# Keys and queries placed by transfers from banks read at full height, and weight sums issued beside the first group

## The chip, the cores and the metric

The kernel runs on one core of one Trainium2 chip, as one launch. The metric is the device time of that core in microseconds, taken as the median of several executions; lower is better. The kernel before took 1184.37 us (median of 3 runs, 1184.14 to 1184.73).

A core has TensorE (PE in the profile), VectorE (DVE), ScalarE (ACT), GpSimd (POOL) and SyncE (SP). They run beside each other and wait for one another through semaphores. Each executes its own instructions in the order in which the program has them, so an instruction that waits holds up everything behind it on its engine. Transfers are issued by SP, ACT or POOL and run by 16 DMA engines.

## What is computed

A trunk of two layers over 1024 tokens of width 1024, all in float32. Each layer is a normalisation with a scale and a shift that depend on a conditioning vector (adaLN), a token mixer, and a gated residual. The reference, cut to the mixers:

```python
def even_mixer(h, ...):                       # layer 0
    qa, ka, va, ga, cq, ckv, kr, gb = split(h @ w_in)
    # first group: 8 query heads over 2 key heads, head size 64, dense softmax
    oa = dense_gqa_attention(axial_rope(rms_norm(qa)), axial_rope(rms_norm(ka)), va)
    # second group: 8 heads, keys and values from a latent of width 128
    qb = rms_norm(cq) @ w_uq                  # 64 columns without, 32 with rotation, per head
    q_lat = einsum('bshd,chd->bshc', q_nope, w_uk)
    ob = mla_attention(q_lat, rope(q_rope), rms_norm(ckv), rope(kr), w_uv)
    return concat([oa * silu(ga), ob * silu(gb)]) @ w_out

def odd_mixer(h, ...):                        # layer 1
    qc, kc, vc, gc = split(h @ w_in)          # 16 query heads, 4 key heads, head size 64
    # each block of 128 queries sees keys at most 128 tokens away, with a distance penalty and a sink
    return (windowed_sink_attention(qc, kc, vc, sink, slopes) * silu(gc)) @ w_out
```

After layer 1 comes a last normalisation.

## The kernel before

**Precision.** A matmul takes float32r, a shorter format than float32. Each operand is therefore held as a high part (its rounding, written by a copy with a float32r output) and a low part (the rest, by `sub`, line 641), and a product is made of three matmuls (`mm3`, line 644: high x high, high x low, low x high). So a projection's PSUM bank is read twice: by a copy on ACT for the high part, and by a subtraction on DVE for the low part.

**Keys and queries at half height.** A head has 64 dimensions, and a tile has 128 partitions. The projection of a pair of heads fills a bank of 128 partitions by 512 tokens: the even head in partitions 0 to 63, the odd head in 64 to 127. The score matmuls get their several products into one contraction by stacking high and low parts in the two halves of a tile, so each part is needed in particular halves of particular tiles. The kernel before writes each of these places straight from the bank, 64 partitions at a time:

- `b_heads` (line 1397), second group, per pair of heads and half of the tokens: three copies on ACT, one on POOL (`K2E`, line 1391) and two subtractions on DVE for the keys (lines 1409 to 1414), and as many for the queries (lines 1420 to 1425). The rotated part of the queries is brought back from DRAM (`qr_sp`) by transfers that POOL issues (lines 1401, 1402).
- `k_ft` (line 1783) and `q_ft` (line 1802), layer 1: four copies and four subtractions for a pair of keys, two and two for a pair of queries.
- `win_PV` (line 1887) adds the two halves of the attention output in four DVE operations of 64 x 128 (line 1906) into `og1`, which has one tile per pair of heads.

**Attention of layer 0.** `run_groups` (line 1183) walks 32 groups: 16 of the first group (head h, half of the queries; `Pa`, `hla` in the profile), then 16 of the second (`Pb`, `hlb`). For a group it makes scores of 128 queries by 1024 keys, takes the maximum on DVE (`nm`), the exponential on ACT, and scales the result by the reciprocal sum on POOL (line 1159). In the next group the result is transposed on PE, split into `hl` on ACT and DVE, and multiplied by the values. `before(n)` (line 1467) adds side work to group n: rotation of queries on POOL (`q_stack_a`, groups 2, 6, 10), preparation of the second group (`B_AT`, line 66), modulation sums (`ADA_AT`, line 71), and the weight sums below.

**Weight sums.** The output projections (`wino_out`, line 1569) use a scheme of seven products of quarter matrices, which needs sums of quarters of the weights. `weight_sums` (line 1458) makes them without an engine's arithmetic: SP loads a quarter into a tile `ws`, POOL issues a transfer that adds another quarter to it, SP stores the sum to DRAM, and this is repeated:

```python
load(t, w(1, 0) if not third else w(0, 0), mark)
for a, b, k in [(3, 1, 0)] if third else [(1, 1, 1), (2, 0, 0), (4, 0, 1)]:
    nc.gpsimd.dma_start(out=t, in_=w(b, k), accum_op=ALU.add)
    nc.sync.dma_start(out=ws_sp[l, a, j], in_=t)
```

Over both layers that is 8 loads, 16 accumulating transfers and 16 stores of 512 KB. `WS_AT` (line 60) puts them at groups 17 to 24.

**What sets the order.** The program is first recorded (`Recorder`, line 115). `run` (line 259) then simulates it with a cost for every operation and a priority that is its place in the recording plus a shift, hands out tiles and banks as they come free, and so gets one order of all instructions, in which they are emitted. A transfer is given a cost at line 416: it begins 1300 ns after its issue or when the one before it is through, moves 410 bytes per ns (205 when it accumulates), and is taken to land 500 ns later (line 417). If the chip is later than the plan, the order stays, and the engine waits.

**Start and tail.** `rstd_rows` (line 742) turns the sums of squares into factors, spread over all partitions by transposes into a bank (line 766). At the start, `warm` (line 695) fills PE's waits with transposes that nobody reads (`WARM`, line 55; the third number are those behind that bank's). The main loop at line 919 normalises one chunk of the input after another. The tail, `finish` (line 1520), multiplies the last outputs by these factors and stores them.

## Time and profile before

| what | value |
|---|---|
| median of 3 runs | 1184.37 us (1184.14 to 1184.73) |
| profiled execution: its time, its span | 1186.49 us, 1184.7 us |
| mean granted clock of TensorE | 0.991 |
| share of DVE, ACT, POOL in the span | 81%, 59%, 51% |
| moved by DMA | 133.44 MB, mean 113 GB/s |
| first group: its scores begin | 138.0 us |
| second group: its scores begin | 423.6 us |
| layer 1's windows: scores | from 786.3 us |

The span goes from the first to the last instruction. A line of the profile names the line of the kernel at which an instruction was emitted; since the order is planned first, nearly all have line 551, and one goes by the names of the tiles: what stands before the arrow is written, what stands behind it is read. "psum" is any bank. "x" is a count. "Idle before" is time in which the engine stood still just before these instructions, with the instruction that ended it. A queue (SPq, POOLq) is the part of an engine that issues transfers.

### The profile page before, as it was taken

What the parts mean: (1) busy time and instruction counts of PE and PEld (TensorE: products, weight loads), DVE (VectorE), ACT (ScalarE), POOL (GpSimd) and SP (SyncE); (2) the same over time, 40 slices, a digit from 0 to 9 for tenths busy, and PEclk for the clock granted to TensorE, in tenths of its full rate; (3) what the DMA queues carried; (4) which work ended last, traced back from release to release, by engine and by line L of the source; (5) the groups of instructions that cost most, each with busy time, mean ns of one, the idle gap of its engine ahead of it and who ended that gap; (6) DMA issues with size and microseconds to landing.
All of it is one profiled execution on the core that took longest, in us unless ns stands there. A gap on an engine that the chain in (4) does not pass through costs nothing.

```text
span 1184.7 us, 17555 instructions
## 1 busy us (share of the span) xinstructions
PE 1144.0 (97%) x6080; PEld 961.5 (81%) x6080; DVE 961.6 (81%) x1743; ACT 699.6 (59%) x1405; POOL 608.0 (51%) x592
## 2 busy tenths in 40 slices
PE   8999999999999999799999999999999999999996
PEld 7898877878878778588878787988888888888885
DVE  8974889888887987678889988968887488776986
ACT  5553356566655777677678842336765366565723
POOL 1344496857855566354436352714465265445424
PEclk9999999999999999999999999999999999999999
DMA  9602423232122189671116343400111122046413
GB/s 370 249 1 72 168 104 124 90 125 93 64 63 82 74 214 247 163 198 38 36 72 240 116 142 113 171 18 2 37 45 63 54 73 72 19 160 228 127 38 142
DMA packets 42441, 133.44 MB, mean 113 GB/s; under 512 B 4592, under 2 KB 9200, under 8 KB 42352
## 3 DMA queue, kind: packets, MB, share of 16 engines
q1 hardware_dynamic: 38192, 120.78, 28.6%
q0 software_dynamic: 3072, 10.49, 4.9%
q8 instruction: 48, 0.79, 0.3%
q10 hardware_dynamic: 1088, 1.05, 0.3%
q14 instruction: 41, 0.34, 0.1%
HBM read 101.24 MB, written 31.06 MB: 112 GB/s over the span
## 4 chain that ended last, share of the span: by engine, by line
PE 78%; DVE 10%; ACT 4%; DMA 3%; issue 2%; POOL 2%; SPq 0%; POOLq 0%; DVEq 0%; ACTq 0%
PE psum L551 78%; DVE nm L551 2%; DMA ws<-in_w_out 2%; DVE p L551 1%; DVE hla L551 1%; DMA ws<-ws 1%; DVE xr L551 1%; ACT Pa L551 1%; DMA xT<-in_xt 1%; ACT q L551 1%; DVE t40l L551 0%; POOL r L551 0%; POOL sq L551 0%; DVE hl L551 0%; ACT p L551 0%
## 5 line engine op out<-in xcount | busy, mean ns | idle before, releaser
L551 DVE TENSOR_REDUCE nm<-psum 128x1 f32<-128x1024 f32 x128 | 154.6, 1216 | 26.4 <-PE psum L551 24.8
L551 POOL TENSOR_SCALAR p<-p,dn 128x384 f32<-128x384 f32 (+1 forms) x128 | 72.5, 587 | 163.1 <-DVE dn L551 85.4
L551 PE MATMUL psum<-hla,VA 128*128 128x512 f32 x256 | 94.4, 428 | 7.9 <-DVE hla L551 5.4
L551 POOL TENSOR_SCALAR Pa<-Pa,rs 128x1024 f32<-128x1024 f32 x64 | 79.0, 1242 | 40.2 <-DVE rs L551 37.5
L551 ACT ACTIVATE Pb<-psum,nm 128x1024 f32<-128x1024 f32 x64 | 71.9, 1125 | 36.0 <-DVE nm L551 30.3
L551 ACT CAST hla<-psum 128x512 fp32r<-128x512 f32 x128 | 71.4, 597 | 37.0 <-PE psum L551 31.2
L551 DVE TENSOR_TENSOR hla<-psum,hla 128x512 fp32r<-128x512 f32 x128 | 83.7, 681 | 11.4 <-ACT hla L551 10.9
L551 PE MATMUL psum<-hlb,VB 128*128 128x512 f32 x256 | 90.6, 426 | 2.2 <-DVE hlb L551 1.5
L551 ACT ACTIVATE Pa<-psum,nm 128x1024 f32<-128x1024 f32 x64 | 71.7, 1122 | 33.6 <-DVE nm L551 28.4
L551 PE MATMUL psum<-ident,Pa 128*128 128x128 f32 x512 | 89.2, 273 | 0.8 <-DVE q L551 0.6
L551 POOL TENSOR_SCALAR Pb<-Pb,rs 128x1024 f32<-128x1024 f32 x64 | 73.3, 1195 | 30.5 <-DVE rs L551 27.6
L551 DVE TENSOR_TENSOR hlb<-psum,hlb 128x512 fp32r<-128x512 f32 x128 | 82.1, 683 | 7.6 <-ACT hlb L551 6.7
L551 PE MATMUL psum<-k,q 128*128 128x512 f32 x256 | 86.2, 408 | 1.0 <-ACT Pb L551 1.0
L551 PE MATMUL psum<-ident,Pb 128*128 128x128 f32 x512 | 79.7, 273 | 7.3 <-POOL Pb L551 6.7
L551 DVE CUSTOM_DVE_ANT_0 p<-psum,bias,rows_g 128x384 f32<-128x384 f32 (+1 forms) x128 | 70.5, 578 | 12.2 <-PE psum L551 10.9
L551 PEld LDWEIGHTS psum<-ident,Pb 128*128 128x128 f32 x512 | 63.2, 140 | 19.4 <-POOL Pb L551 7.3
L551 ACT ACTIVATE p<-p,nm 128x384 f32<-128x384 f32 (+1 forms) x128 | 74.1, 585 | 7.7 <-DVE nm L551 7.7
L551 ACT COPY ot<-psum 64x512 f32<-64x512 f32 x64 | 37.4, 584 | 65.2 <-PE psum L551 64.5
L551 ACT CAST hlb<-psum 128x512 fp32r<-128x512 f32 x128 | 69.2, 604 | 10.2 <-PE psum L551 7.8
L551 PEld LDWEIGHTS psum<-ident,Pa 128*128 128x128 f32 x512 | 64.2, 141 | 11.9 <-DVE q L551 0.8
L551 PEld LDWEIGHTS psum<-hla,VA 128*128 128x128 f32 x256 | 46.7, 191 | 20.6 <-DVE hla L551 9.4
L551 ACT CAST hl<-psum 128x512 fp32r<-128x512 f32 x88 | 46.6, 593 | 27.9 <-PE psum L551 22.0
(891 smaller groups left out, 3671.1 us busy)
## 6 DMA issues: line engine op xcount, KB each, us to landing
ada<-in_ada_t SPq DMA_DIRECT2D x32, 512.0 KB, 7.1
adag<-in_ada_t SPq DMA_DIRECT2D x16, 512.0 KB, 4.9
ws<-in_w_out POOLq DMA_DIRECT2D x16, 512.0 KB, 6.2
ws<-ws SPq DMA_DIRECT2D x16, 512.0 KB, 3.1
S<-ws SPq DMA_DIRECT2D x16, 512.0 KB, 4.4
o<-spill SPq DMA_DIRECT2D x12, 512.0 KB, 5.8
A<-in_w_out SPq DMA_DIRECT2D x12, 512.0 KB, 5.8
xT<-in_xt SPq DMA_DIRECT2D x8, 512.0 KB, 8.1
```

Of the source, the lines that this page charges most:

```text
L551: fn(*[real(v) for v in a], **{k: real(v) for k, v in kw.items()})
```

## The change

1. `WS_AT` puts the weight sums at groups 2 to 9 in place of 17 to 24, and the planner takes an accumulating transfer to land 3000 ns after its move in place of 500.
2. A new helper, `two_parts`, reads a whole bank of 128 partitions once on ACT (high) and once on DVE (low) into a tile of its own. `put` then brings a half of it to its place by a transfer on SP. `b_heads`, `k_ft` and `q_ft` use them: twelve transfers of 64 x 512 per call of `b_heads`, eight per call for the keys and four for the queries of layer 1. The transfers from `qr_sp` are issued by SP in place of POOL.
3. In layer 1 the tiles `og1` and `g1` hold a half of the tokens for two pairs of heads in place of all tokens for one pair; `win_PV` adds in two operations in place of four, the spills go out by half, and `wino_out` takes the kept ones as whole tiles.
4. At the start, 8 in place of 20 warming transposes stand behind the first factors, and the copy of these factors out of their bank comes after the first chunk. In the tail, the last factors are spread into two banks, one is copied by ACT, and one of the four last products is made by POOL from the copy.

The diff, cut to its core:

```diff
-WARM = (32, 14, 20)
+WARM = (32, 14, 8)
-WS_AT = {17: ((0, 0, False),), 18: ((0, 0, True),), 19: ((0, 1, False),), 20: ((0, 1, True),),
-         21: ((1, 0, False),), 22: ((1, 0, True),), 23: ((1, 1, False),), 24: ((1, 1, True),)}
+WS_AT = {2: ((0, 0, False),), 3: ((0, 0, True),), 4: ((0, 1, False),), 5: ((0, 1, True),),
+         6: ((1, 0, False),), 7: ((1, 0, True),), 8: ((1, 1, False),), 9: ((1, 1, True),)}
...
-                        fin = dma_free + 500
+                        fin = dma_free + (3000 if "accum_op" in o.call[2] else 500)
...
+    def two_parts(ps, name, scale=None):
+
+        t = UR(name)
+        h, l = t[:, 0:512], t[:, 512:1024]
+        if scale is None:
+            nc.scalar.copy(h, ps)
+            sub(l, ps, f(h))
+        else:
+            nc.scalar.activation(h, ps, AF.Copy, scale=scale)
+            nc.vector.scalar_tensor_tensor(out=l, in0=ps, scalar=scale, in1=f(h), op0=ALU.mult, op1=ALU.subtract)
+        return [[x[e * 64:(e + 1) * 64, :] for x in (h, l)] for e in range(2)]
+
+    def put(o, i):
+        nc.sync.dma_start(out=f(o), in_=f(i))
...
+        if kc == 0:
+            rb0 = rows_copy(rp0, "x0")
...
-            nc.gpsimd.dma_start(out=q1[h][64:96, :], in_=qr_sp[0][h * 32:(h + 1) * 32, :])
-            nc.gpsimd.dma_start(out=q1[h][96:128, :], in_=qr_sp[1][h * 32:(h + 1) * 32, :])
+            nc.sync.dma_start(out=f(q1[h])[64:96, :], in_=qr_sp[0][h * 32:(h + 1) * 32, :])
+            nc.sync.dma_start(out=f(q1[h])[96:128, :], in_=qr_sp[1][h * 32:(h + 1) * 32, :])
...
-        nc.scalar.copy(k1[0][0:64, c], ps[0:64, :])
-        nc.scalar.copy(k2[o][64:128, c], ps[64:128, :])
-        nc.scalar.copy(k1[1][0:64, c], ps[64:128, :])
-        K2E(k2[e][0:64, c], f(k1[0][0:64, c]))
-        sub(k2[e][64:128, c], ps[0:64, :], f(k1[0][0:64, c]))
-        sub(k2[o][0:64, c], ps[64:128, :], f(k2[o][64:128, c]))
+        (he, le), (ho, lo) = two_parts(ps, f"knp{p}{half}")
+        for d, r, x in ((k1[0], 0, he), (k2[e], 0, he), (k2[e], 64, le), (k1[1], 0, ho), (k2[o], 64, ho), (k2[o], 0, lo)):
+            put(d[r:r + 64, c], x)
...
-                        r_ = pr if last else rb
-                        (nc.vector if last else nc.gpsimd).tensor_tensor(
+                        dve = last and k2 != 2
+                        r_ = pr if dve else rb
+                        (nc.vector if dve else nc.gpsimd).tensor_tensor(
...
-            for e in range(2):
+            for e, (h, l) in enumerate(two_parts(ps, f"k1p{p}{half}")):
                 g = 2 * p + e
                 if half == 0:
                     kh1[g], kl1[g] = UR(f"kh1{g}"), UR(f"kl1{g}")
...
+                for r in (0, 64):
+                    put(kh1[g][r:r + 64, c], h)
+                    put(kl1[g][r:r + 64, c], l)
...
+            Q = Q1[p, half] = UR(f"Q1{p}{half}")
+            for e, (h, l) in enumerate(two_parts(ps, f"Q1p{p}{half}", 0.125)):
+                put(Q[e * 64:(e + 1) * 64, e * 512:(e + 1) * 512], h)
+                put(Q[64 - e * 64:128 - e * 64, e * 512:(e + 1) * 512], l)
...
-        for j in range(4):
-            r = slice((j % 2) * 64, (j % 2) * 64 + 64)
-            nc.vector.tensor_tensor(out=og[j // 2][r, i * P:(i + 1) * P], in0=acc[0:64, j * P:(j + 1) * P],
-                                    in1=tmp[:, j * P:(j + 1) * P], op=ALU.add)
+        o = og[i // 4].rearrange("p (a c) -> p a c", a=2)
+        by = lambda t: t.rearrange("p (a e c) -> p a e c", a=2, e=2)
+        for e in range(2):
+            nc.vector.tensor_tensor(out=o[e * 64:(e + 1) * 64, :, (i % 4) * P:(i % 4 + 1) * P],
+                                    in0=by(acc[0:64, :])[:, :, e, :], in1=by(tmp)[:, :, e, :], op=ALU.add)
```

More of the change, by code (lines that the diff above doesn't have):

```diff
@@ L763, in rstd_rows @@
         marks["rstd", name] = nc.gpsimd.tensor_tensor(out=r[:, 0:nt], in0=v, in1=mhalf[:, 0:nt], op=ALU.pow)
-        pr = PA(f"rb{name}")
-        for j in range(nt):
-            m_ = nc.tensor.transpose(out=pr[:, j * P:(j + 1) * P], in_=r[:, j:j + 1].broadcast_to([P, P]), identity=ident)
+        prs = [PA(f"rb{name}{k}") for k in range(2 if twice else 1)]
+        for pr in prs:
+            for j in range(nt):
+                m_ = nc.tensor.transpose(out=pr[:, j * P:(j + 1) * P], in_=r[:, j:j + 1].broadcast_to([P, P]),
+                                         identity=ident)
         if name == "x0" and WARM[2]:
             warm(WARM[2], m_)
-        return pr[:, 0:n]
+        return [pr[:, 0:n] for pr in prs] if twice else pr[:, 0:n]
     def rows_copy(pr, name):
@@ L1520, in finish @@
         def finish(res, half, c0, n, pr, last):
-            if not last:
+            if last:
+                pr, p2 = pr
+                rb = rows_copy(p2, f"z{half}{c0}")
+            else:
                 rb = rows_copy(pr, f"z{half}{c0}")
@@ L1559, in after @@
             if pos == 7:
-                finish(res, half, c0, n, rstd_rows(sums, f"z{half}{c0}"), last)
+                finish(res, half, c0, n, rstd_rows(sums, f"z{half}{c0}", last), last)
         return after
@@ L1575, in raw_o @@
         def raw_o(half, k2, mark):
+            if (half, k2) in kept:
+                s = kept[half, k2]
+                return [None, s[:, 0:512], s[:, 512:1024]]
             gone = [e for e in range(2) if 2 * k2 + e not in kept]
@@ L1824, in evac @@
             nc.gpsimd.tensor_tensor(out=sl, in0=sl, in1=t, op=ALU.mult)
-            if half == 1 and p < 6:
-                spill_out(1, p, og1.pop(p))
+            if p % 2 and p < 6:
+                nc.sync.dma_start(out=spill[4 + p // 2][half], in_=og1[p // 2][half])
         return proj_ft(10 + p, f"g1f{p}", evac)
@@ L1941, in encoder_kernel @@
         win_bias(g)
-        for j in range(2):
-            og1[2 * g + j] = U(f"og1{g}{j}")
+        og1[g] = [U(f"og1{g}{half}") for half in range(2)]
         for i in range(NT):
@@ L1958, in encoder_kernel @@
     assert not halves
-    for j in (6, 7):
-        nc.gpsimd.tensor_tensor(out=og1[j], in0=og1[j], in1=g1[j], op=ALU.mult)
-        keep[j] = og1[j]
+    for half in range(2):
+        o = keep[half, 3] = og1[3][half]
+        for e in range(2):
+            c = slice(e * 512, e * 512 + 512)
+            nc.gpsimd.tensor_tensor(out=o[:, c], in0=o[:, c], in1=g1[half][:, c], op=ALU.mult)
     wino_out(1, w_out1, keep, [("w", 3, 3), ("w", 3, 4), ("w", 3, 5), ("w", 3, 6)], x1_sp, layer1_after())
```

44 lines of the change are left out of this document (10 added, 34 removed).

## The prediction

> **What bounds the kernel.** I read the page first: is one engine full, and where is it not?
>
> ```profile
> span 1184.7 us, 17555 instructions
> PE 1144.0 (97%) x6080; PEld 961.5 (81%) x6080; DVE 961.6 (81%) x1743; ACT 699.6 (59%) x1405; POOL 608.0 (51%) x592
> ```
>
> PE is the bound and its matmuls stay (only twelve warming transposes go and two come), so no more can be won than PE's idle time, 1184.7 - 1144.0 = 40.7 us, and what is lost at a lowered clock. Next the view of stretches, for the stages that the change touches. After the stretch come its length, the busy times of PE, PEld, DVE, ACT and POOL with their counts, the granted clock, the DMA share and GB/s.
>
> ```profile
> 25.00:50.00 25.00, 25.00 (x122) 22.46 (x122) 24.05 (x36) 17.07 (x20) 0.67 (x1) 1.00 0.94 370
> 150.00:175.00 25.00, 23.01 (x114) 18.69 (x113) 20.79 (x35) 14.24 (x28) 24.16 (x21) 0.95 0.24 93
> 150.00:275.00 125.00, 118.63 (x617) 95.90 (x616) 109.04 (x166) 74.53 (x137) 91.00 (x81) 0.97 0.29 99
> 400.00:660.00 260.00, 245.63 (x1317) 198.55 (x1316) 218.15 (x343) 194.23 (x356) 136.44 (x137) 0.99 0.51 145
> 500.00:525.00 25.00, 23.81 (x115) 19.50 (x116) 17.24 (x26) 13.84 (x26) 15.42 (x15) 0.86 0.77 187
> 770.00:1080.00 310.00, 308.42 (x1629) 262.89 (x1628) 237.67 (x673) 181.18 (x469) 142.04 (x179) 1.00 0.17 57
> ```
>
> The second group (400 to 660) leaves PE idle for 14.4 us, layer 1's windows (770 to 1080) only 1.6. So the many edits in layer 1 can hardly pay, and the argument is about the second group. Third, PE's waits, and PE's and POOL's timelines around the longest (start, length, engine, what, and in brackets the idle time before it with its releaser); SP's rows stand with them.
>
> ```profile
> PE psum L551 <- POOL Pb L551: 6.7, 2, 5.9
> 501.19 0.47 PE L551 MATMUL psum<-ident,Pb 128*128 128x128 f32 x1 [5.92 <-POOL Pb L551]
> 501.32 1.20 PE L551 MATMUL psum<-k,q 128*128 128x512 f32 x2
> ...
> 507.31 0.39 PE L551 MATMUL psum<-krl,q 128*128 128x512 f32 x1
> 507.54 0.63 PE L551 MATMUL psum<-k,q 128*128 128x512 f32 x2
> ```
>
> ```profile
> 499.06 0.88 POOL L551 DMA_DIRECT2D ws<-in_w_out  x1 [9.21 <-DMA ws<-in_w_out]
> 471.19 22.26 SPq L551 DMA_DIRECT2D ws<-ws  x4
> 493.56 1.21 SPq L551 DMA_DIRECT2D ws<-in_w_out  x2
> ```
>
> This is one chain over three queues. SP spends 22.26 us on four stores of weight sums, each waiting for an accumulating transfer to land; the load behind them starts at 493.56; POOL's next accumulation waits for that load until 499.06; the normalisation of Pb stands behind it on POOL; PE waits for that, 5.9 us. Then the clock is down: between 501.32 and 507.31 lie 14 matmuls, 0.428 us each, where 507.31 to 507.54 shows 0.23; 14 x (0.428 - 0.23) = 2.8 us more, and the row from 500 shows the granted clock at 0.86. The stall costs 5.9 + 2.8 = 8.7 us. Last, the chain of waits through the second group, its shares of 260 us:
>
> ```profile
> by line: PE psum L551 65.3%; DMA ws<-in_w_out 8.9%; issue 3.7%; DMA ws<-ws 3.1%; DVE nm L551 2.8%; ACT q L551 2.3%; ACT Pb L551 1.9%; DVE hlb L551 1.6%; DVE q L551 1.5%; POOL Pb L551 1.4%; DVE b110l L551 1.2%; ACT hlb L551 1.2%; ACT k L551
> ```
>
> Evacuations of queries alone hold 2.3% + 1.5%, 9.9 us: the copies in the heads' preparation do reach the chain.
>
> **1. Weight sums to groups 2 to 9.** Eight loads and sixteen stores on SP and sixteen accumulations on POOL move as they are, past POOL's query rotations, low parts of gate weights and Pa normalisations, and past SP's loads of gate and modulation weights and queries. All of PE's waits for Pb were seen in the second group (6.7); with the clock loss they go: -(6.7 + 2.8) = **-9.5 us**. What they cost anew:
>
> ```profile
> L551 POOL DMA_DIRECT2D ws<-in_w_out x16 | 14.5, 904 | 34.7 <-DMA ws<-in_w_out 11.2 <-DMA ws<-ws 10.6 <-DVE hlb L551 6.3
> ws<-in_w_out POOLq DMA_DIRECT2D x16, 512.0 KB, 6.2
> ws<-in_w_out SPq DMA_DIRECT2D x8, 512.0 KB, 5.3
> ```
>
> POOL is busy 91.0 of 125 us where they come to lie, and 105.5 with their 14.5; that fits. The wait is the danger: whatever stands behind a waiting accumulation on POOL waits too, the Pa tiles first, and PE's transposes for those. The planner now lets an accumulation land 3.0 us after its move instead of 0.5: by its own arithmetic (1.3 + 512 KB at 205 B/ns, 2.6, + 3.0) 6.9 us, above the 6.2 measured, where it assumed 4.4. So stores stop jamming SP. For a plain load it still assumes 1.3 + 1.3 + 0.5 = 3.1 against 5.3, so the first accumulation of each of the eight tiles can hold POOL some 2.2 us. POOL's first-group rows show slack for a few of these; nearest rows for the bounds are nothing, and one stall like the above, 8.7. I take **+1.5 us**, near the lower end, since of the two waits for loads (11.2 us) only the 9.2 one made PE wait 5.9.
>
> **2. Heads of the second group.** Rows for half and full height:
>
> ```profile
> L551 ACT CAST k<-psum 64x512 fp32r<-64x512 f32 x24 | 14.0, 582 | 2.3 <-PE psum L551 2.0
> L551 ACT CAST hlb<-psum 128x512 fp32r<-128x512 f32 x128 | 69.2, 604 | 10.2 <-PE psum L551 7.8 <-issue 0.8 <-DMA ws<-ws 0.5
> L551 DVE TENSOR_TENSOR k<-psum,k 64x512 fp32r<-64x512 f32 x16 | 11.0, 688 | 5.0 <-ACT k L551 4.7
> L551 DVE TENSOR_TENSOR hlb<-psum,hlb 128x512 fp32r<-128x512 f32 x128 | 82.1, 683 | 7.6 <-ACT hlb L551 6.7
> L551 POOL TENSOR_SCALAR k<-k 64x512 fp32r<-64x512 f32 x12 | 8.6, 719 | 4.6 <-ACT k L551 4.3
> ```
>
> Full height costs what half height costs. Each of eight calls drops from six copies to two on ACT (3.49 to 1.21), from four subtractions to two on DVE (2.75 to 1.37), and loses two copies on POOL (1.44): over the stage 18 us of ACT, 11 of DVE, 11.5 of POOL. Sixteen query transfers leave POOL's queue for SP's. Of PE's 14.4 idle us, 14.4 - 6.7 = 7.7 are not POOL's; they stand behind DVE and ACT, where these copies queue among the exponentials and hlb. I take half, **-4.0 us**; ends 0 and -7.7.
>
> New are 96 transfers of 128 KB on SP, twelve a call, waiting on DVE and ACT. Behind a waiting one stand only SP's other loads; who waits for them is the scores' matmul. No such transfer within the memory of the engines is in the trace; nearest rows, and the place with the least margin:
>
> ```profile
> kr_sp<-krraw SPq DMA_DIRECT2D x1, 128.0 KB, 1.7
> q<-qr_sp POOLq DMA_DIRECT2D x16, 128.0 KB, 4.6
> L551 SPq DMA_DIRECT2D ropeb<-kr_sp x1: 423/423/423, 321.2 to 321.2; - x1
> 422.34 0.70 DVE q L551
> L551 PE MATMUL psum<-k,q x256: 387/389/774, 423.6 to 655.6; 128*128 128x512 f32 x128
> ```
>
> Twelve issues at 0.42 are 5.1 us, landing lies between 1.7 and 4.6. The first head's last subtraction ends at 423.04 and its scores start at 423.60; later heads are prepared a group ahead (a group lasts 260/16, 16 us) and are covered. So once, transfers come behind the subtraction: 1.7 us for one, 5.1 + 4.6 = 9.7 for a whole call's, less the 2.28 + 1.38 = 3.7 us by which a call got shorter on ACT and DVE, and PE has PV products to fill with. A gain is excluded, since only waits are added: ends 0 and 6.0. I take **+1.5 us**, layer 1's first query included, by the first row: these transfers too are issued by SP.
>
> [...]
>
> **3. Layer 1.** Keys and queries go from two or four half-height pieces to one full pair, PV's four sums of 128 columns to two of 256 (0.42 by the line through 283 ns at 128 and 688 at 512 columns):
>
> ```profile
> L551 ACT ACTIVATE Q<-psum 64x512 fp32r<-64x512 f32 x32 | 19.0, 593 | 22.9 <-PE psum L551 17.3 <-issue 5.0 <-POOL p L551 0.4
> L551 DVE SCALAR_TENSOR_TENSOR Q<-psum,Q 64x512 fp32r<-64x512 f32 x32 | 22.0, 689 | 17.6 <-ACT Q L551 17.1
> L551 DVE TENSOR_TENSOR kl<-psum,kh 64x512 fp32r<-64x512 f32 x16 | 11.0, 688 | 8.1 <-ACT kh L551 7.9
> L551 DVE TENSOR_TENSOR og<-psum,ot 64x128 f32<-64x128 f32 x128 | 36.2, 283 | 18.9 <-ACT ot L551 17.3
> ```
>
> DVE saves 11.0 + 8.3 + 9.4 = 28.7 us of 237.7, beside a PE that idles 1.6: **-1.0 us**, ends 0 and -1.6. Its 96 transfers meet a DMA share of 0.17. Spills by half instead of by column keep their bytes and lie under the same cover.
>
> **4. Start and tail.**
>
> ```profile
> 15.59 4.01 PE L551 MATMUL psum<-ident 128*128 128x128 f32 x20
> 16.51 0.59 ACT L551 COPY rbx<-psum 128x512 f32<-128x512 f32 x1 [1.69 <-DVE xT L551]
> 19.36 0.44 PE L551 MATMUL psum<-w10h,hT00h 128*128 128x416 f32 x1
> 1178.19 2.48 DVE L551 TENSOR_TENSOR xr<-xr,psum 128x512 f32<-128x512 f32 x4 [1.31 <-PE psum L551]
> ```
>
> Eight transposes instead of twenty end at 17.2 (0.2 each), and the copy no longer precedes the first chunk, ready 0.59 earlier: PE can begin near 17.3, 2.1 us sooner. But DVE, which feeds it, is busy 24.05 of 25 us from 25 to 50, with work that stays: **-0.5**, ends 0 and -2.1. In the tail DVE makes three products of 0.62 instead of four, POOL one beside it after a copy: **-0.4**, ends +0.5 and -0.6.
>
> **Sum.** -9.5 + 1.5 - 4.0 + 1.5 - 1.0 - 0.5 - 0.4 = -12.4 us. The profiled execution took 1186.49 us, 1.8 over its span, and 2.1 over the median 1184.37. Span 1184.7 - 12.4 = 1172.3; profiled 1174.1; median **1172.0**. A measurement tells about 0.2% (2.4 us) from no change. Best ends together: -9.5 - 7.7 - 1.6 - 2.1 - 0.6 = -21.5, so 1163.
>
> **Rivals.** *One POOL stall returns in the first group.* For: the planner's 3.1 against 5.3 on eight loads, POOL at 24.16 of 25 from 150 to 175. Against: slack on average. -12.4 - 1.5 + 8.7 = -5.2: 1179; chance 0.16. *Transfers come late* at the first head: the term of 1.5 becomes 6.0, the sum -7.9: 1176; chance 0.10. [...] *No change:* the weight sums slide back behind the first group for want of free tiles, or both of these eat the gain: 1183; chance 0.07. *Slower:* accumulations hold POOL in the first group two or three times, each stall 8.7 us with its lowered clock. From two on the change loses: -13.9 + 17.4 = +3.5 gives 1188, three give 1197. For it speaks that the queries' rotation there sits on POOL too; against, that the planner's new landing time takes out the cause of the stall in the trace. Chance 0.13. The forecast keeps 0.54.
>
> **Numbers.** Faster by over 0.2%: 0.54 + 0.16 + 0.10 = 0.80; within 0.07; slower 0.13. From 1163 to 1186 leaves out the slower rival and little below. The forecast's own range is 1165 to 1177.
>
> **What would show it.** Right: in 400 to 660 PE's waits for Pb under 1 us and PE idle near 4 to 5; POOL's accumulations between 150 and 290, waits for DMA under 10 us in all; ACT's and DVE's k and q pieces replaced by 16 at full height on each; PE's first projection near 17.3. Wrong: a wait of over 3 us of PE for Pa with a DMA of ws on POOL ahead of it; a DMA of k or q releasing PE; PE's idle in the second group still above 10 us; or layer 1 gaining more than 1.6.

## The result and the profile after

The changed kernel takes 1195.51 us (median of 6 runs, 1188.60 to 1196.37) where the kernel before took 1184.55 on the same chip (6 runs, 1182.71 to 1187.59): ratio 1.0074, 95% interval 1.0048 to 1.0100. It is 0.7% slower; 1.0% faster was forecast. The six times lie in two bunches, two near 1188.8 us and four near 1195.9, so that the medians are 0.9% apart; the profiled execution, 1196.02 us, is one of the upper bunch. That of the kernel before took 1186.49, 1.9 over its median, so the spans are only 9.5 us apart.

Where the time went shows when the span is cut at five matmuls of PE: the first scores of the first group, of the second group, the first output projection, the first windows of layer 1, and the last matmul of the second output projection (each by its start).

| us | start | first group | second group | projection, layer 1's first part | windows, second projection | tail | span |
|---|---|---|---|---|---|---|---|
| before | 137.98 | 285.62 | 243.88 | 119.01 | 387.29 | 10.94 | 1184.72 |
| after | 138.60 | 299.19 | 236.18 | 120.86 | 388.05 | 11.37 | 1194.25 |
| difference | +0.6 | +13.6 | -7.7 | +1.8 | +0.8 | +0.4 | +9.5 |

The second group gains most of the 9.5 us that were forecast for the weight sums there. The first group, where they now lie, loses nearly twice as much. The marks are not quite equal in work: thirteen of the first group's last matmuls (ten transposes and three products, some 1.6 us by the spacing of such rows) lie behind the second mark in the kernel after, so the first loss is rather larger and the gain too. The first lines of the page after, and the same stretches of after as were shown of before (the second group and layer 1 moved by the 14 and 10 us that they now come later):

```profile
span 1194.2 us, 17832 instructions
PE 1146.9 (96%) x6070; PEld 962.0 (81%) x6070; DVE 922.7 (77%) x1634; ACT 664.5 (56%) x1346; POOL 592.9 (50%) x563
```

```profile
0.00:25.00 25.00, 18.94 (x98) 16.91 (x99) 19.20 (x33) 13.59 (x19) 3.18 (x9) 0.86 0.92 362
...
150.00:175.00 25.00, 19.80 (x90) 15.96 (x89) 18.52 (x21) 10.16 (x19) 16.43 (x16) 0.86 0.59 199
150.00:275.00 125.00, 110.11 (x549) 87.61 (x548) 102.98 (x147) 68.36 (x124) 92.34 (x88) 0.95 0.78 229
414.00:674.00 260.00, 249.77 (x1374) 205.66 (x1375) 213.12 (x340) 180.91 (x336) 108.26 (x93) 0.99 0.40 115
780.00:1090.00 310.00, 308.28 (x1604) 260.95 (x1603) 204.42 (x583) 165.97 (x446) 143.26 (x178) 1.00 0.33 95
```

Between 150 and 275 PE is busy 110.1 us at a clock of 0.95, where it was 118.6 at 0.97. POOL, which the prediction feared for, is busy 92.3, hardly more than the 91.0 of before. DVE saves 33 us in layer 1 (204 for 238), and PE's busy share there is as before: that saving bought nothing.

PE's waits in the first group, up to the second group's first scores, of after and then of before (us in total, times, longest):

```profile
PE psum L551 <- ACT Pa L551: 7.0, 10, 2.8
PE psum L551 <- DVE hla L551: 5.7, 4, 5.2
PE psum L551 <- DMA q<-qr_sp: 3.6, 1, 3.6
PE psum L551 <- ACT hla L551: 2.7, 2, 2.3
PE psum L551 <- DVE gT L551: 2.1, 1, 2.1
```

```profile
PE psum L551 <- DVE hla L551: 4.6, 6, 1.7
PE psum L551 <- ACT Pa L551: 4.5, 5, 1.9
```

No row names POOL. The 3.6 us for `q<-qr_sp` are the wait for the second group's first head; it ends at the mark and so counts in the 299.19. The longest wait is for DVE's `hla`. Its stretch on the timelines of POOL, DVE, PE and SP (start, length, engine, what, idle before it):

```profile
156.68 0.93 POOL L551 DMA_DIRECT2D ws<-in_w_out  x1 [1.55 <-DVE hla L551]
157.35 2.52 POOL L551 TENSOR_SCALAR Pa<-Pa,rs 128x1024 f32<-128x1024 f32 x2
159.54 2.63 POOL L551 TENSOR_TENSOR wg1l<-wg1s,wg1h 128x1024 fp32r<-128x1024 f32 x1
161.85 1.32 POOL L551 TENSOR_TENSOR qp<-qp,r 128x512 f32<-128x512 f32 x1
163.24 2.02 POOL L551 TENSOR_TENSOR nrq<-qp,qtab 128x256 f32<-128x256 f32 x2
```

```profile
156.94 7.32 DVE L551 CUSTOM_DVE_ANT_0 ada<-ada,cb,a 128x1024 f32<-128x1024 f32 x1
...
164.19 1.88 DVE L551 TENSOR_TENSOR hla<-psum,hla 128x512 fp32r<-128x512 f32 x3
```

```profile
159.33 0.40 PE L551 MATMUL psum<-hT01h,wg4l 128*128 128x512 f32 x1
164.92 1.22 PE L551 MATMUL psum<-hla,VA 128*128 128x512 f32 x2 [5.20 <-DVE hla L551]
```

```profile
149.22 13.22 SPq L551 DMA_DIRECT2D ws<-ws  x2
SPq L551 <- DMA ws<-in_w_out: 77.6, 14, 11.7
```

A modulation sum of DVE (`ada`; the group's median is 1.3 us) begins 0.26 us behind an accumulation that POOL has issued, and takes 7.32 us: it ends 1.1 us after `qp`, the fourth operation of POOL's row behind the accumulation. The subtractions for `hla` stand behind it, and PE waits 5.2 us for those. Two more sums in this trace, at 206.2 and 221.9, take 4.27 and 3.63 us beside accumulations, ahead of PE's waits of 2.8 and 2.1.

The last two rows are SP. Two stores of weight sums hold its queue for 13.22 us. The first leaves at once and lands at 156.1, 6.9 us after its issue; the second accumulation, which adds to the same tile, cannot begin before that and leaves POOL at 156.68; the second store waits until 162.1 for this accumulation. In all, SP stands 77.6 us of the first group until an accumulation has landed, 14 times. What stands behind such a store comes late. The chain that ended last (start, us, what) shows it for the second of the long sums:

```profile
192.24 8.41 DMA ws<-in_w_out
201.08 4.91 DMA ada<-in_ada_t
206.16 4.27 DVE ada L551
```

An accumulation lands, the store that waited for it leaves SP, behind it the load for a modulation sum, and the sum begins when this load has landed, just beside the next two accumulations (205.19 and 205.76).

### The profile page after: what moved, and what is told of

Its sections match the earlier page's. It is cut to its first block, busy times and chain, and to the rows that moved or that the text cites. A ratio compares the mean times of both kernels' runs of the same rounds, so it can differ in the third digit from the quotient of the medians.

```text
span 1194.2 us, 17832 instructions
## 1 busy us (share of the span) xinstructions
PE 1146.9 (96%) x6070; PEld 962.0 (81%) x6070; DVE 922.7 (77%) x1634; ACT 664.5 (56%) x1346; POOL 592.9 (50%) x563
## 4 chain that ended last, share of the span: by engine, by line
PE 76%; DVE 9%; DMA 4%; ACT 3%; issue 3%; POOL 2%; SPq 1%; POOLq 0%; ACTq 0%; DVEq 0%
PE psum L551 76%; DVE nm L551 2%; DMA ws<-in_w_out 1%; SPq L551 1%; DVE hla L551 1%; ACT Pa L551 1%; DVE ada L551 1%; DVE xr L551 1%; DMA Q<-Q1p 1%; DMA xT<-in_xt 1%; POOL r L551 1%; DVE t40l L551 0%; POOL sq L551 0%; DMA ada<-in_ada_t 0%; ACT hla L551 0%
## 5 line engine op out<-in xcount | busy, mean ns | idle before, releaser
L551 PE MATMUL psum<-hlb,VB 128*128 128x512 f32 x256 | 87.6, 419 | 2.1 <-DVE hlb L551 2.1
L551 DVE TENSOR_TENSOR hl<-psum,hl 128x512 fp32r<-128x512 f32 x88 | 55.7, 684 | 10.1 <-ACT hl L551 9.5
```

The costliest lines, as they stand in the source:

```text
L551: fn(*[real(v) for v in a], **{k: real(v) for k, v in kw.items()})
```

## Theory and rival

Two mechanisms could carry the loss. **SP:** accumulations land late, stores wait for them on SP, loads and further accumulations behind these stores come late, and POOL's and DVE's work slides into places that were not planned. **POOL and DVE:** an accumulation issued by POOL makes DVE's sums long, whatever SP does. The forecast's own rival, POOL held by waiting accumulations, had already lost: POOL waited for a transfer of weights once, 7.3 us, and PE for POOL not at all.

## The experiments

e1, e2, e3 and e6 keep the changed kernel's order and alter transfers, e13 moves one with its store; the others, but for the repeat e8, are planned anew. The table gives the stage lengths of those that are compared by stage.

| us | first group | second group | projection, layer 1's first part | windows, second projection | median | ratio to before, 95% |
|---|---|---|---|---|---|---|
| e2 plain copies by POOL | 284.61 | 235.50 | 120.60 | 388.02 | 1180.06 | 0.9963 (0.9948 to 0.9978) |
| e4 weight sums back | 282.69 | 246.36 | 120.74 | 388.25 | 1190.20 | 1.0035 (1.0016 to 1.0055) |
| e5 weight sums alone | 300.08 | 233.67 | 118.85 | 387.49 | 1190.11 | 1.0050 (1.0033 to 1.0068) |
| e6 stores that do not wait | 284.46 | 236.20 | 120.70 | 388.05 | 1180.74 | 0.9971 (0.9962 to 0.9980) |
| e7 sums spread | 284.10 | 236.58 | 121.05 | 393.24 | 1185.37 | 1.0018 (1.0008 to 1.0028) |
| e9 later landings | 292.11 | 236.04 | 120.84 | 388.20 | 1188.26 | 1.0026 (1.0014 to 1.0038) |
| e10 e5, later landings | 290.26 | 233.74 | 119.11 | 387.23 | 1183.09 | 0.9984 (0.9975 to 0.9994) |
| e11 e9, heads early | 288.67 | 233.85 | 119.08 | 388.09 | 1181.41 | 0.9965 (0.9953 to 0.9978) |
| e12 layer 1 alone | 283.41 | 242.25 | 120.74 | 388.09 | 1185.37 | 1.0010 (1.0001 to 1.0020) |
| e13 one accumulation later | 299.88 | 235.13 | 120.59 | 387.98 | 1195.97 | 1.0092 (1.0074 to 1.0110) |
| e14 e11, modulation late | 284.96 | 234.03 | 119.11 | 387.98 | 1177.83 | 0.9940 (0.9923 to 0.9956) |
| e15 e10, modulation late | 288.19 | 238.48 | 118.81 | 387.16 | 1184.96 | 0.9999 (0.9988 to 1.0011) |
| e16 e14, layer 1 as before | 284.87 | 234.01 | 117.32 | 387.23 | 1175.67 | 0.9919 (0.9904 to 0.9934) |

**e1, e2: what the accumulations cost.** In both the sixteen accumulations become plain copies (the sums are left out), issued by SP in e1 and still by POOL in e2; the edit of e1:

```diff
-                fn, a, kw = o.call
+                fn, a, kw = o.call if "accum_op" not in o.call[2] else (self.nc.sync.dma_start, (), dict(out=o.call[2]["out"], in_=o.call[2]["in_"]))
```

> The changed kernel with its planned order kept on every engine; only the 16 accumulating transfers of the weight sums are issued by SP in place of POOL, at their old places in the program, and as plain copies (the sums are left out, so each stored quarter is the one copied last). Theory A (the first group's new stalls come from DVE's two-operand sums of the modulation, which do not get through while POOL works back to back behind an accumulation's issue): the three long modulation sums of the changed kernel (7.31, 4.27 and 3.63 us against 1.3) shrink to under 2.4 us, the scores of the second group begin near 427 to 430 in place of 437.8, the time falls by 7 to 10 us to 1186 to 1189. Rival B (SP is jammed by stores that wait for slow accumulations, so the loads behind them are late for DVE): copies land sooner than accumulations, so part comes back, but SP now also holds the 16 issues and their waits; long sums stay long where DVE waits for its load, time 1190 to 1196. Rival C (the new order as such is worse, whatever its transfers): 1195 as before, stalls at the same places.

> The changed kernel with the same order on every engine and every queue; the 16 transfers of the weight sums still go out from POOL, but as plain copies (the sums are left out). Theory A: POOL's issue stays, so the long modulation sums stay (one over 5 us, two over 3) and the time stays at 1189 to 1196. Rival B: copies land 2 to 3 us sooner, SP's stores let go sooner, the modulation loads are in time, and at least half of the 13.6 us lost in the first group comes back: 1186 to 1189. Rival C: unchanged, 1195.

e1 took 1177.29 us (ratio 0.9933, 0.9914 to 0.9952); it has a time and no trace that can be read by stage. e2 took 1180.06. So 15 of the 18 us that e1 wins over the changed kernel come with the kind of transfer, not with the engine that issues it. A plain copy on POOL's queue lands in 5.0 us, an accumulation in 7.2:

```profile
ws<-in_w_out POOLq DMA_DIRECT2D x16, 512.0 KB, 5.0
```

```profile
ws<-in_w_out POOLq DMA_DIRECT2D x16, 512.0 KB, 7.2
```

The first row is e2's, the second the changed kernel's. With the earlier landings the first group is back at 284.6, although POOL issues as many transfers. The form "any transfer issued by POOL costs this" falls. How little decides at 156 us: in e2 POOL issues at 156.63, as late as in the changed kernel, but the sum begins at 156.41, ahead of it, and takes 1.33 us.

**e3: rotated queries loaded on POOL again.**

```diff
+                fn, a, kw = o.call if not (... in_ is qr_sp ...) else (self.nc.gpsimd.dma_start, (), o.call[2])
```

> The changed kernel with the same order on PE, DVE and ACT; only the 16 transfers that bring the rotated queries back from DRAM are issued by POOL again in place of SP. If the wait of 3.6 us before the second group's first scores (and the lowered clock behind it, 2.2 us) comes from SP's queue of placing transfers, the scores begin 3 to 5 us sooner after the last work of the first group and the time falls by 4 to 6 us. If it comes from the chain through DRAM itself (stores at 424 to 427, landing, load), the wait stays within 1 us and the time does not move.

1196.91 us (ratio 1.0091, 1.0064 to 1.0119), first group 299.50, second 238.12: no gain. The expectation tied an unmoved time to an unmoved wait, and missed there: PE's wait of 3.6 us for these loads is gone, and other waits stand in its place. PE waits 1.6 us for ACT's `hla` and 0.5 for a placing transfer. POOL waits 7.5 us until the stores of the rotated queries have landed, with the Pa tiles behind it. So the queue that loads these queries decides which wait PE shows, and not when the second group begins; this run does not single out what does.

**e4, e5: the parts.** e4 is the changed kernel with `WS_AT` as before; e5 is the kernel before with `WS_AT` and the landing of 3000 ns as after, and nothing else.

> The changed kernel with the weight sums at groups 17 to 24 again, planned anew; all else of the change stays, the planner's 3.0 us for accumulations too. Theory A and rival B: the first group loses what it lost before (second group's scores begin at 424 to 428 plus the wait for the rotated queries), the second group may lose some of its gain; 1179 to 1186. Rival C (the rest of the change is what costs): 1190 to 1196.

> The kernel before with the weight sums alone moved to groups 2 to 9 and the longer landing in the planner; heads, layer 1, start and tail as before. Theory (accumulations that land late hold SP's stores and loads and POOL, so the first group loses what the second gains): the second group's scores begin 10 us or more later than in the kernel before, and the whole comes to 1183 to 1192. Rival (the loss came out of the whole replanning, the new heads and start among it, and not out of the move): the move alone gives the 9.5 us that were forecast, 1173 to 1178, and the second group's scores begin within 3 us of the kernel before.

e5 shows the move by itself: second group -10.2 us, first group +14.5, all else within 0.2. The longest of its waits are the changed kernel's:

```profile
PE psum L551 <- DVE hla L551: 8.0, 6, 5.2
PE psum L551 <- ACT Pa L551: 6.5, 9, 3.1
```

The rival, that the replanning of the rest had done it, falls. e4 shows the rest without the move: first group -2.9, second +2.5, layer 1 and the stretch ahead of it +2.7. From e4 to the changed kernel, which differ in `WS_AT` alone, the first group loses 16.5 and the second gains 10.2. In its second group the placing transfers now stand on SP with the stores of weight sums:

```profile
PE psum L551 <- DMA q<-qnp: 3.7, 2, 2.9
PE psum L551 <- POOL Pb L551: 2.9, 2, 2.6
PE psum L551 <- DMA q<-qr_sp: 2.4, 1, 2.4
```

**e6: stores that wait for nothing.** The order is kept; the stores read a weight matrix in DRAM.

```diff
+                fn, a, kw = o.call if not (... a store of ws ...) else (o.call[0], (), dict(out=o.call[2]["out"], in_=self.free))
```

> The changed kernel with its order kept on every engine and queue; only what the sixteen stores of weight sums read is changed: a weight matrix in DRAM, so that they wait for no accumulation (the sums that the output projections read are then not the sums). The accumulations stay, with their traffic and their landing. Theory (the late landing costs through SP: its stores wait, and the modulation loads behind them are late): the stalls at 209.7 and 261.8 go, and the first group gets 5 us or more of its 13.6 back; about 1186 to 1190. Rival (it costs through POOL and DVE: long modulation sums beside POOL's accumulations): the first group stays within 2 us of the changed kernel, and the time at 1193 to 1196.

1180.74 us. The first group falls from 299.2 to 284.5, while the sixteen accumulations, their order and their traffic stay; they even land later, after a median of 8.6 us. This breaks the alternation on both sides: no store waits for an accumulation, and no accumulation for a store (the sums that are stored are then not the sums). The loss hangs on that chain. At the first stall, the second accumulation leaves at 154.59, 2.1 us sooner, and the sum at 156.56 takes 1.33. A sum of 3.9 us beside two accumulations is left, at 208.9.

**e7: weight sums spread out.** Layer 0's at groups 3, 7, 11 and 12, layer 1's inside layer 1's windows.

```diff
+WS_AT = {3: ((0, 0, False),), 7: ((0, 0, True),), 11: ((0, 1, False),), 12: ((0, 1, True),)}
+WS_W = {(0, 2): (1, 0, False), (0, 6): (1, 0, True), (1, 2): (1, 1, False), (1, 6): (1, 1, True)}
...
+            if (g, i) in WS_W:
+                weight_sums(*WS_W[g, i], marks["w", g, i])
```

> The changed kernel with the weight sums of layer 0 at groups 3, 7, 11 and 12 of the first group, one in three or four groups in place of one in each, and those of layer 1 in layer 1's windows (two in the first window row, two in the second), planned anew. Theory (the number of accumulations that lie close together beside the first group decides): the first group loses under 4 us against the kernel before, the second keeps its gain of about 7 us, layer 1 loses under 2; about 1176 to 1182. Rival (any accumulation beside the first group costs as much as in the changed kernel, 13.6 us for sixteen): half of the loss stays, 1186 to 1189.

1185.37 us. The first group is at 284.1 with half as many accumulations, but the windows lose 5.2 us, where the theory allowed 2: PE there waits for placing transfers (1.8 us on `Q<-Q1p`); the rest was not followed up. One sum of 5.0 us remains in its first group, at 259.1, 37 us behind the nearest accumulation ahead of it, inside a row of four POOL operations.

**e8: the changed kernel again.**

> The changed kernel as it is, for a second profile: its times lie in two bunches, 1188.6 to 1188.9 and 1195.0 to 1196.4. Theory (the bunches differ by whether the modulation sum at 156.9 runs into POOL's row of operations): a time of 1188.6 to 1188.9 comes with a sum of under 3 us there and no stall of PE at 159, and a time of 1195 to 1196 with the sum of 7.3 us and the stall. Rival (another place, or the clock): the profile of a time near 1188.7 has the stall at 159 all the same.

One time, 1194.84 us, with the sum at 156.6 taking 7.3 us and the stall at 159. It fell into the upper bunch again; what sets the lower one stays open. That e2's sum escapes by beginning 0.2 us ahead of POOL's issue, where the changed kernel's comes 0.26 behind it, would fit two bunches 7 us apart, but no trace of the lower one exists.

**e9, e10: a plan with later landings.**

```diff
-                        fin = dma_free + (3000 if "accum_op" in o.call[2] else 500)
+                        fin = dma_free + (5000 if "accum_op" in o.call[2] else 3500 if ... load of ws ... else 500)
```

> The changed kernel, planned anew with the transfers of the weight sums taken to land later: loads 3500 ns after their move in place of 500, accumulations 5000 in place of 3000; nothing else is changed. Theory (stores that wait on SP for accumulations, and loads late behind them, are the loss): the planner now puts stores and accumulations where they find their data, the second group's scores begin within 3 us of the kernel before (423.6) and the time is 1178 to 1183, as with the stores that wait for nothing. Rival (the work itself, sixteen accumulations and their traffic, is too much for the first group, wherever they are put): the scores begin after 430, 1187 or more.

> The kernel before with its old heads, layer 1, start and tail, the weight sums moved to groups 2 to 9, and the same later landings (3500 and 5000 ns) in the planner. Theory (the move is worth what was forecast as soon as SP is not held, and the new heads bring nothing): the second group is 10 us shorter than in the kernel before, as in the move alone, and the first group at most 2 longer; 1174 to 1178, under the changed kernel with the same landings by 3 us or more. Rival (the new heads bring their 4 us of forecast): 1183 or more, above the changed kernel with the same landings.

1188.26 and 1183.09 us. The stalls at 159, 210 and 224 are gone, half or more of the first group's loss with them (292.1 and 290.3). A new one of 4.4 and 4.6 us stands at 179, behind a sum of 5.3 and 5.8 us. POOL, then DVE, in e9:

```profile
173.53 1.80 POOL L551 DMA_DIRECT2D ws<-in_w_out  x2
174.76 3.91 POOL L551 TENSOR_SCALAR Pa<-Pa,rs 128x1024 f32<-128x1024 f32 x3
178.05 4.59 POOL L551 TENSOR_TENSOR nrq<-qp,qtab 128x256 f32<-128x256 f32 x6
```

```profile
177.04 5.31 DVE L551 CUSTOM_DVE_ANT_0 ada<-ada,cb,cols 128x1024 f32<-128x1024 f32 x1
```

So later landings in the plan do not undo the chain as e6 did: SP still stands 58.3 us for accumulations in e9's first group (77.6 in the changed kernel), and POOL's row meets a sum of DVE at another place.

**e11: the second group prepared one group earlier**, on top of e9. Its start, its rotated keys and queries and both calls for the first pair of heads move, five numbers of the list:

```diff
-B_AT = (14, 13, 14, 15, 15, 15, 19, 19, 22, 23, 27, 27, 23)
+B_AT = (13, 12, 13, 15, 14, 14, 19, 19, 22, 23, 27, 27, 23)
```

> The changed kernel with the same later landings and with the second group's start, its rotated keys and queries one group earlier, and the first pair of heads of the second half of the tokens too (three numbers of the list of places one lower, a fourth likewise). Theory (the first head waits because the rotated queries go out to DRAM and come back late on SP): the wait of PE for those loads, 3 to 4 us with 2 us of lowered clock behind it, shrinks under 1 us, and the time is 3 to 5 us under the kernel with only the later landings. Rival (SP is the limit there, or other work takes the place): within 1.5 us of it.

1181.41 us, 6.9 under e9. The wait for `q<-qr_sp` is gone from PE's waits; first group -3.4, second -2.2, which is that wait (3.8) and the lowered clock behind it. The stretch ahead of layer 1's windows is 1.8 shorter too, for a reason that was not followed up.

**e12: layer 1's part alone**, on the kernel before.

> The kernel before with layer 1's part of the change alone: keys and queries placed by transfers, tiles by half, two additions in place of four. Theory (the placing transfers come late for the first windows, and an idle DVE is worth nothing there): the stretch from the output projection of layer 0 to the first window's scores is 1.8 us longer, and the windows gain nothing; 1.5 to 3 us slower than the kernel before. Rival (the prediction's term): 1 us faster, up to 1.6.

1185.37 us, ratio 1.0010 (1.0001 to 1.0020). The two stretches of layer 1 are 1.7 and 0.8 us longer, as the theory said; the two groups of layer 0 are 3.8 shorter by the two profiled executions, part of which is that the one of before lay 1.9 us over its median, so the whole came out smaller than expected.

**e13: one accumulation moved**, the second, behind the six POOL operations that followed it; its store moves behind the next load on SP.

> The changed kernel with one accumulation, the second (at 156.7 us), put behind the six POOL operations that followed it; its store on SP changes places with the load behind it, and the order of all else is kept. Theory (a modulation sum of DVE that begins right behind an accumulation issued by POOL waits out the whole row of POOL's operations behind it): the sum at 156.9 takes 1.3 to 2.5 us in place of 7.3, PE's stall of 5.4 us at 159 and the lowered clock behind it go, 5 to 7.5 us off the changed kernel, 1187 to 1190. Rival (POOL's row holds DVE whatever stands ahead of it): the sum stays over 5 us and the time over 1193.

The sum took 1.32 us in place of 7.32. But the time stayed, 1195.97 us, so the expectation for the whole missed. DVE, POOL, and PE's waits in e13:

```profile
156.36 1.32 DVE L551 CUSTOM_DVE_ANT_0 ada<-ada,cb,a 128x1024 f32<-128x1024 f32 x1
```

```profile
156.54 2.14 POOL L551 TENSOR_SCALAR Pa<-Pa,rs 128x1024 f32<-128x1024 f32 x1 [0.17 <-DVE rs L551]
...
164.09 0.91 POOL L551 DMA_DIRECT2D ws<-in_w_out  x1
164.78 1.54 POOL L551 TENSOR_TENSOR og('0', 0)_321<-og('0', 0)_321,gT 64x512 f32<-64x512 f32 x1
173.14 0.87 POOL L551 DMA_DIRECT2D ws<-in_w_out  x1 [6.81 <-DMA ws<-ws]
```

```profile
PE psum L551 <- POOL Pa L551: 4.9, 2, 4.3
```

The third accumulation now waits 6.8 us for the store of the second; the Pa tiles stand behind it on POOL, and PE waits 4.3 us for them. That is the wait the prediction had feared, made here by moving one transfer. The sum in e13 also began 0.18 us ahead of POOL's next operation, and it was now POOL that waited: this Pa operation took 2.14 us, the one ahead of it 1.13. So this run shows that the accumulation's place decides, but not by which of the two, the transfer in front or who begins first.

**e14, e15, e16: modulation sums away from the accumulations**, at groups 11, 12, 13, 17 and 18; e14 on e11, e15 on e10, e16 is e14 with layer 1 as before.

```diff
-ADA_AT = (8, 5, ("c2", 6), 2, 4, 10, ("op", 1, 7), ("w", 2, 2))
+ADA_AT = (17, 18, ("c2", 6), 11, 12, 13, ("op", 1, 7), ("w", 2, 2))
```

> The kernel with later landings and the early start of the second group, with the modulation sums of groups 2, 4, 5, 8 and 10 at groups 11, 12, 13, 17 and 18, where POOL issues hardly any accumulation. Theory: no sum there takes over 3 us, the stall of 4.6 us at 179 and its lowered clock go, and the first group gets 5 to 7 us shorter; with what the second group loses to the loads, 1174 to 1179. Rival (DVE has no room there, or the placing transfers come late behind the loads): within 1.5 us of the kernel without the move, 1180 to 1183.

> The kernel before with its old heads, layer 1, start and tail, the weight sums at groups 2 to 9 with later landings, and the modulation sums moved likewise. Theory (the moved sums are the rest of the loss; the new heads bring nothing): 5 to 7 us under the same kernel with the modulation sums in place (1183.1), 1176 to 1179, and not above the new heads' kernel with the same moves by more than 1 us. Rival (the heads bring their 4 us): 3 us or more above it.

> The same kernel as the one with moved modulation sums and the new heads, with layer 1 as in the kernel before (half-height copies, four additions). Theory (placing transfers cost layer 1's first windows 1.8 us and the windows get nothing back): 1 to 2.5 us under the kernel with layer 1's part, and the fastest of all. Rival: layer 1's part gains its 1.0 us as forecast, and this is 1 us slower.

e14 takes 1177.83 us, 3.6 under e11. Its longest sum is 2.34 us, and of the first group's waits none is over 1.1:

```profile
PE psum L551 <- ACT Pa L551: 6.2, 13, 1.1
PE psum L551 <- DVE hla L551: 1.8, 4, 0.8
PE psum L551 <- DVE cqTl L551: 1.0, 1, 1.0
```

So the long sums were the rest of the loss, by the stall of 4.4 us that went with them; their loads left SP's queue together with them, and how much of the 3.6 that made is not shown. e15 missed: its plan put three sums and a low part on DVE ahead of the one that PE waited for, a stall of 5.1 us at 377, so it says little of the heads. e16 is the fastest of all kernels here, 1175.67 us, ratio 0.9919 (0.9904 to 0.9934), 2.2 under e14. Its two groups of layer 0 run at the full clock:

```profile
138.00:423.00 285.00, 274.31 (x1468) 220.00 (x1466) 229.23 (x366) 172.89 (x323) 196.65 (x193) 1.00 0.56 163
423.00:657.00 234.00, 228.29 (x1268) 188.76 (x1268) 202.34 (x322) 166.42 (x308) 104.11 (x84) 1.00 0.41 126
```

## Why the prediction was wrong

**The step that failed** is the second term of the weight sums: "I take +1.5 us, near the lower end". It measured +14.5 alone (e5) and +16.5 between e4 and the changed kernel, above even the upper end of 8.7. The prediction had looked at one engine, POOL, whether it has room and whether its waiting accumulations hold the Pa tiles. Room it had. What was not costed is that the first group holds 21 modulation sums on DVE (one of them runs into it), none of which lay near an accumulation in the kernel before, and that SP, which must load for these sums, also carries the stores. "So stores stop jamming SP" was wrong too: SP stood 77.6 us for accumulations in the first group. Not the accumulations' landing alone made it so. At the first jam they landed after 5.7 and 5.4 us, sooner than the 6.9 of the plan, while the store between them took 6.9, where the planner's arithmetic for a plain transfer, 3.1, was left as it was. With 2 us more for accumulations and 3 more for loads (e9) half of the loss went; with stores that wait for nothing (e6) all of it.

**The slower rival** had the right sign and range (1188 to 1197), with a chance of 0.13, but not the mechanism: POOL was not held, so its range was hit by luck. Its mechanism is real, as e13 shows, but the plan had kept clear of it.

**The gain of 9.5** in the second group was right: 10.2 in e5. PE waited for POOL's Pb no more.

**Heads, -4.0:** the copies fell as counted, and 16 pieces at full height stand on ACT and on DVE. The gain did not come in the changed kernel: its second group is 2.5 us longer than e5's. Where the first head's wait is taken away on one side (e11) and old heads stand on the other (e10), the second groups agree, 233.85 and 233.74; e11's holds nine matmuls more that the first group left over, about 1 us. So the end of the range at 0 was nearly right: of the forecast 4.0 about 1 is there at most, and these copies were not what PE waited for.

**Late transfers, +1.5:** the place was right, the first head, and the size was at the end of 6.0: a wait of 3.6 us and some 2.2 at a lowered clock behind it (by e11; in the changed kernel the granted clock is 0.50 from 438 to 442). Not the last subtraction set it, but the rotated queries. SP's queue and PE's wait:

```profile
419.85 4.00 SPq L551 DMA_DIRECT2D k<-knp  x5
423.95 1.03 SPq L551 DMA_DIRECT2D qr_sp<-qrh  x2
425.08 2.06 SPq L551 DMA_DIRECT2D qr_sp<-qrl  x2
...
431.26 1.04 SPq L551 DMA_DIRECT2D q<-qr_sp  x2
432.39 1.75 SPq L551 DMA_DIRECT2D q<-qnp  x3
434.19 1.06 SPq L551 DMA_DIRECT2D q<-qr_sp  x2
```

```profile
437.79 1.19 PE L551 MATMUL psum<-k,q 128*128 128x512 f32 x2 [3.60 <-DMA q<-qr_sp]
```

The last stores of the rotated queries had landed at 431.8 by the trace; the loads that wait for them left SP at 434.2, behind three placing transfers, and the first of them landed at 437.55, and PE begins at 437.79. e3, which takes these loads off SP, shows that other parts come just as late, and e11, which prepares all of it one group earlier, takes the wait away. e11 keeps all the placing transfers, which land after 2.3 and 2.4 us by the medians as in the changed kernel, and loses the wait, so their rate does not force it; the rate itself no run here isolates.

**Layer 1, -1.0:** it cost 2.2 us (e14 against e16). The stretch ahead of the first windows is 1.8 longer, but 1.4 of that is work that has moved: six matmuls of the key projection, 0.23 us each, come ahead of the first window's scores in place of behind them. The windows, with these six fewer, are 0.8 longer all the same. The rows of PE's waits there sum to under 3 us, spread over pieces of 0.3 to 0.5; a single cause was not found. **Start, -0.5:** the first projection began at 17.30, as forecast, but the clock in the first 25 us was 0.86 where it had been 0.93 (in e2 and e14, with the same start, it was 1.00), and the first group started 0.6 later; in the other kernels with this start the difference is within 0.25. **Tail, -0.4:** 0.4 longer. These three sizes were small, and none of the gains came.

## What to carry to other kernels

Before work is moved beside another stage, list what that stage has on every engine and queue that the moved work shares with it, here DVE's sums beside POOL's row, and SP's loads, and not only whether the engine that issues it has room. A transfer chain that alternates between two queues (accumulate, store, accumulate) held each queue here until the other's transfer had landed (SP 77.6 us of the first group, POOL 6.8 us at one place of e13), and all that stood behind it: cost every link of it, the stores too. When two changes lean on the same gap, move one of them: here the 10 us of the second group became a gain of the whole only after the modulation sums had made way.

## What the runs showed of the hardware

A modulation sum of DVE (in the changed kernel 1.34 and 1.29 us by the medians of its two forms) took up to 7.32 us there beside POOL. In the traces here 20 modulation sums of the first group take over 3.5 us (7.32, 4.27 and 3.63 in the changed kernel, 5.31 in e9); 19 of them have a transfer issued by POOL within 3 us of their start or inside them (18 times an accumulation, in e2 a plain copy), one has not (e7, 5.0 us). In the three traces whose first group has no accumulation near these sums (before, e4, e12) none of 63 takes over 3.3 us. Each of the 20 ends 1.08 or 1.09 us after an operation of POOL has ended (at 156.94: `qp` ends at 163.17, the sum at 164.26). So they waited for POOL; they were not slow from end to end. One of the longest in the kernel before, POOL and then DVE:

```profile
193.60 2.40 POOL L551 TENSOR_TENSOR wg5l<-wg5s,wg5h 128x1024 fp32r<-128x1024 f32 x1
```

```profile
193.81 3.27 DVE L551 CUSTOM_DVE_ANT_0 ada<-ada,cb,cols 128x1024 f32<-128x1024 f32 x1
```

This one waits out the POOL operation that runs when it begins, 2.2 us, and ends 1.08 us after it. In e13, where the sum begins 0.18 us ahead of POOL's operation, the sum takes 1.32 and POOL's operation 2.14. At 156.94 one POOL operation does not make up the 7.32 us: the sum waited out an issue and four POOL operations. Why it does not get in between them there stays open: in the kernel before a sum that begins at 297.22, inside the first of three Pa operations in a row (from 296.81), takes 1.81 us, ends 1.07 us after that first one, and the second takes 2.12.

An accumulating transfer of 512 KB landed 7.2 us after its issue (the median of 16 in the changed kernel) where a plain one of the same queue and size landed after 5.0 (the median of 16 in e2). A transfer of 128 KB inside the memory of the engines, over 64 partitions, landed after 2.4 us (the median for `k<-knp`); nothing of the kernel before can be set beside it, since its two transfers of that size on SP, 1.7 and 2.7 us, are a store to DRAM and a load from it.
